# The opening of a two-layer backbone: chunk 0's copy, the low parts of the pooling weight, the residual's halves and the first gate weight in another order

## The chip, the core and the metric

The kernel runs on one core of a Trainium2 chip. The metric is the device time of one execution in microseconds (us). Three executions of the kernel before took 3039.23 to 3043.47 us, median 3042.01. One more was profiled.

## The reference, cut to what matters

Two layers over 256 latent tokens and 256 context tokens of 2048 channels, everything in float32. The opening of layer 0 is what the change touches:

```python
ml = (silu_c @ w_mod[i] + b_mod[i]).reshape(B, 6, 1, D)      # shift, scale, gate (mixer); shift, scale, gate (MLP)
a_lat = modulate(rms_norm(h, norm1_g[i]), ml[:, 0], ml[:, 1])
y_lat = pool_mix(a_lat, pool_w[j], pool_b[j], pool_scale[j]) # layer 0; layer 1 is neighbourhood attention
h = h + ml[:, 2] * y_lat
h = h + ml[:, 5] * conv_ffn(modulate(rms_norm(h, norm2_g[i]), ml[:, 3], ml[:, 4]), w_gate, w_up, conv_w, conv_b, w_down)
```

`pool_mix` takes, in each of four groups of 512 channels, the mean over a window of 2, 4, 8 or 16 tokens less the token itself, multiplies it with the group's 512x512 weight, and adds a bias. The context goes the same way with its own modulation.

## The kernel before, in words

**Layout.** Channels lie on the 128 partitions, so an activation is 16 tiles of 128 channels, each with 256 latent columns (`hl`, stream 0) and 256 context columns (`hc`, stream 1). Every float32 product is made of three: a weight is cast into a high part (`h` at the end of its name) on ScalarE (ACT) and a low part (`l`, the rest) on VectorE (DVE), activations likewise, and TensorE (PE) sums high x high, high x low and low x high into one PSUM bank. `load` (L132) brings 128x1024 tiles of 512 KB through SyncE's DMA queue; `split` (L148, L150) makes the two parts. A staged tile takes one of 15, later 14, rooms in rotation, so that a load waits until the tile that had its room has been used up.

**Modulation.** `w_mod` of layer 0 comes in chunks of 512 outputs: chunks 0 to 3 are the mixer's shift, 4 to 7 its scale, 8 to 11 its gate, 12 to 15 the MLP's shift, 16 to 19 its scale. A chunk has eight tiles (`wm_8_2_1024` is the second half of group 2 of chunk 8). `mod_pe` multiplies each tile on TensorE (L184, 32 columns at a time, four rows of the profile for one tile), copies the bank out on ACT (L191, `modev`), transposes it (L196, `modt`), and VectorE sums it (L199), adds the bias (L170) and, for scales, multiplies with the norm's gain (L172). The result is a column of numbers per chunk, `modT`.

**The first group's mixer.** `mixer(0)` makes the pooled rows `pf` of four tiles before the modulation is known (L567, L575, L576), casts the pooling weight (`parts = ld(wp[0], ...)`), multiplies the rows with chunk 4's scale on ACT (L625) and adds chunk 0's shift on VectorE (L626), and splits them (`ph`: L580 on ACT, L581 on VectorE). TensorE then makes 4 x 4 x 3 = 48 products of 512 columns (L588 to L590) into four banks, `pm_0` to `pm_3`. With chunk 8 known (`gsc`, `gbi`, L647 and L649), each bank is scaled (L663 on VectorE for the latent half, L666 on ACT for the context half) and added to the stream (L668, on VectorE or GpSimd). With chunk 16 known, the stream becomes the MLP's input `Ad` (L678 on ACT, L679 on VectorE).

**The gate and up products.** `partial(g, ...)` multiplies the four `Ad` tiles of group g with the first eight column tiles of the gate and up weights: `cg_0` to `cg_7`, `cu_0` to `cu_7` (L742 to L744), with small products for the shifts (`pw`, L698). The first gate weight `wcg_0` is loaded and split ahead, as `ahead`. Between the products, `between` calls `need`, which lets the loads and products of further chunks be recorded, and steps the mixer of the next group.

**What sets the order.** The program is recorded by generators that are stepped by hand (the loop over `(0, 8, 11, 13, 17, 17, 17)`: `need(n)` records the products of chunks up to a count of groups, `next(mix)` records the next piece of the mixer), and a scheduler then lays the instructions on each engine's queue by their priority and their own readiness in its model. Within an engine, and on SyncE's queue, instructions go in the order so fixed. `tc.issue_after(x)` keeps instructions behind x, `tc.high_priority()` moves them ahead.

## Time and profile before

| what | value |
|---|---|
| median of 3 runs | 3042.01 us |
| the profiled execution | 3042.44 us |
| its span, first to last instruction | 3040.7 us |
| TensorE busy | 2972.1 us, 98% |
| VectorE busy | 2054.5 us, 68% |
| ACT busy | 1347.4 us, 44% |
| HBM read | 563.32 MB, 189 GB/s over the span |

Rows of the timeline read: start, length, engine, line, operation, what is written and read, shape, how many, and in brackets how long the engine stood idle before and what released it. Rows of the chain of waits have start, length and name. A row of the waits gives the total, the number and the longest. A window's row gives the busy time of TensorE, its weight loads, VectorE, ACT and GpSimd, then the granted TensorE clock, the DMA share and GB/s. Times count from the first instruction.

### The profile page before, as it was taken

The page shows a single profiled execution, that of the slowest core. Times are in us where ns is not written, and L with a number is a line of the kernel's source. Part 1 is how long each engine was busy: PE and PEld are TensorE (multiplying, and loading weights), DVE is VectorE, ACT ScalarE, POOL GpSimd, SP SyncE. Part 2 cuts the span into 40 slices and gives each one's busy share as a digit, 9 for nine tenths or more (in the row PEclk, how much of TensorE's full clock was granted, in tenths as well). Part 3 has the DMA queues.
Part 4 walks back from the last instruction along what each step waited for, and adds up shares of the span by engine and source line. Part 5 has one row for each costly group of instructions (what it writes and reads, how often), then busy time and mean ns, then how long its engine had stood idle before and what let it go on. Part 6 is the DMA issues. An engine that isn't in the chain of part 4 may idle for free.

```text
span 3040.7 us, 40895 instructions
## 1 busy us (share of the span) xinstructions
PE 2972.1 (98%) x14846; PEld 2399.2 (79%) x14846; DVE 2054.5 (68%) x2894; ACT 1347.4 (44%) x2205; POOL 884.4 (29%) x868
## 2 busy tenths in 40 slices
PE   6999999999999999999999999999999999999998
PEld 2565678887888888888887888888888888888887
DVE  5445887576876867587686666474867666666666
ACT  3333473323334232333334444343546666566665
POOL 1111320303213030322413111010102566566665
PEclk9999999999999999999999999999999999999999
DMA  9878635454866857676783333333355555555563
GB/s 376 326 279 322 218 97 171 157 185 157 254 195 193 260 174 243 201 235 205 215 240 101 112 109 109 103 113 104 112 165 181 180 192 191 192 181 189 183 195 113
DMA packets 224778, 572.31 MB, mean 188 GB/s; under 512 B 55232, under 2 KB 68032, under 8 KB 224576
## 3 DMA queue, kind: packets, MB, share of 16 engines
q1 hardware_dynamic: 224576, 569.70, 58.0%
q8 instruction: 117, 1.92, 0.3%
q14 instruction: 85, 0.70, 0.1%
HBM read 563.32 MB, written 11.53 MB: 189 GB/s over the span
## 4 chain that ended last, share of the span: by engine, by line
PE 89%; issue 3%; DVE 3%; DMA 2%; ACT 1%; POOL 1%; SPq 0%; DVEq 0%; ACTq 0%; POOLq 0%
PE g L1018 5%; PE u L1018 5%; PE d L900 5%; PE d L902 5%; PE d L901 5%; PE d L1068 4%; PE u L865 4%; PE u L863 4%; PE u L864 4%; PE g L865 4%; PE g L864 4%; PE g L863 4%; PE u L1021 3%; PE g L1021 3%; PE d L1072 2%
## 5 line engine op out<-in xcount | busy, mean ns | idle before, releaser
L921 POOL TENSOR_TENSOR hl<-hl,dy 128x256 f32<-128x256 f32 x144 | 146.2, 1015 | 941.8 <-ACT dy L918 676.8
L1085 POOL TENSOR_TENSOR hl<-hl,dy 128x256 f32<-128x256 f32 x320 | 327.1, 1057 | 188.5 <-ACT dy L1083 186.2
L270 DVE SCALAR_TENSOR_TENSOR macc<-wm,sc,macc 128x512 f32<-128x512 f32 x360 | 262.3, 780 | 9.0 <-DMA wm<-wmod 8.9
L248 DVE SCALAR_TENSOR_TENSOR macc<-wm,sc,macc 128x1024 f32<-128x1024 f32 x120 | 160.4, 1336 | 87.3 <-DMA wm<-wmod 86.1
L918 ACT ACTIVATE dy<-d,modT 128x256 f32<-128x256 f32 x224 | 93.6, 471 | 138.6 <-PE d L902 134.7
L921 POOL TENSOR_TENSOR hc<-hc,dy 128x256 f32<-128x256 f32 x144 | 141.4, 982 | 0.0
L1261 POOL COPY bias<-rows 128x160 f32<-128x160 f32 x64 | 37.1, 579 | 306.2 <-issue 195.6
L1083 ACT ACTIVATE dy<-d,modT 128x512 f32<-128x512 f32 x160 | 104.5, 684 | 42.8 <-PE d L1072 41.3
L184 PE MATMUL mod<-wm,sc 128*32 128x512 f32 x640 | 101.6, 616 | 21.2 <-DVE n1q L353 18.9
L150 DVE TENSOR_TENSOR wd_2l<-wd,wd_2h 128x1024 fp32r<-128x1024 f32 (+1 forms) x44 | 58.6, 1343 | 60.5 <-ACT wd_2h L148 60.5
L488 ACT ACTIVATE sg<-g 128x512 f32<-128x512 f32 x43 | 27.3, 634 | 146.0 <-DVE g L485 145.9
L150 DVE TENSOR_TENSOR wd_3l<-wd,wd_3h 128x1024 fp32r<-128x1024 f32 (+1 forms) x44 | 54.5, 1262 | 52.7 <-ACT wd_3h L148 52.7
L575 POOL TENSOR_TENSOR pf<-ws,inv 128x256 f32<-128x256 f32 x32 | 27.9, 894 | 204.4 <-DVE ws L567 131.9
L148 ACT CAST wd_0h<-wd 128x1024 fp32r<-128x1024 f32 (+1 forms) x44 | 45.3, 1032 | 79.5 <-PE g L864 51.0
L150 DVE TENSOR_TENSOR wd_1l<-wd,wd_1h 128x1024 fp32r<-128x1024 f32 (+1 forms) x44 | 55.3, 1259 | 31.6 <-ACT wd_1h L148 31.6
L184 PEld LDWEIGHTS mod<-wm,sc 128*32 128x32 f32 x640 | 18.4, 109 | 65.1 <-issue 32.7
L1044 DVE TENSOR_TENSOR actb<-sgb,actb 128x256 fp32r<-128x256 f32 x43 | 52.9, 1229 | 23.7 <-ACT actb L1043 23.7
L900 PE MATMUL d<-act,wd_0h 128*128 128x512 f32 x172 | 67.4, 395 | 1.0 <-ACT dy L918 1.0
L900 PE MATMUL d<-act,wd_3h 128*128 128x512 f32 x172 | 68.2, 396 | 0.0
L901 PE MATMUL d<-act,wd_2h 128*128 128x512 f32 x172 | 68.1, 396 | 0.0
L150 DVE TENSOR_TENSOR wd_0l<-wd,wd_0h 128x1024 fp32r<-128x1024 f32 (+1 forms) x44 | 53.8, 1226 | 21.0 <-ACT wd_0h L148 21.0
L902 PE MATMUL d<-act,wd_0l 128*128 128x512 f32 x172 | 67.9, 395 | 0.0
(1708 smaller groups left out, 9381.7 us busy)
## 6 DMA issues: line engine op xcount, KB each, us to landing
wm<-wmod SPq DMA_DIRECT2D x384, 512.0 KB, 6.2
wd<-wd SPq DMA_DIRECT2D x168, 512.0 KB, 4.5
wg<-wg SPq DMA_DIRECT2D x156, 512.0 KB, 4.6
wu<-wu SPq DMA_DIRECT2D x156, 512.0 KB, 4.5
wv<-wv SPq DMA_DIRECT2D x32, 512.0 KB, 3.7
wk<-wq SPq DMA_DIRECT2D x32, 512.0 KB, 3.7
wq<-wq SPq DMA_DIRECT2D x32, 512.0 KB, 3.7
wo<-wo SPq DMA_DIRECT2D x32, 512.0 KB, 4.4
```

The lines of the kernel that those rows point to most:

```text
L150: eng.tensor_tensor(lo[:, :n], t[:, :n], hi[:, :n].bitcast(F32), op=ALU.subtract)
L270: nc.vector.scalar_tensor_tensor(acc[:, s], w, sc2[:, k, s : s + 1], acc[:, s], op0=ALU.mult, op1=ALU.add)
L863: nc.tensor.matmul(ps, hi[:, c : c + P], xh, start=(k == 0), stop=False)
L864: nc.tensor.matmul(ps, hi[:, c : c + P], xl, start=False, stop=False)
L865: nc.tensor.matmul(ps, lo[:, c : c + P], xh, start=False, stop=(k == KT - 1))
L900: nc.tensor.matmul(ps, hi[:, o : o + P], xh, start=(i == 0), stop=False)
L901: nc.tensor.matmul(ps, hi[:, o : o + P], xl, start=False, stop=False)
L902: nc.tensor.matmul(ps, lo[:, o : o + P], xh, start=False, stop=(i == n - 1))
L921: nc.gpsimd.tensor_tensor(h_of(s)[:, k, :], h_of(s)[:, k, :], y[:, s], op=ALU.add)
L1018: nc.tensor.matmul(ps, hi[:, c : c + P], flat(B[k]), start=(k == 0), stop=False)
L1021: nc.tensor.matmul(ps[:, T:], lo[:, c : c + P], B[k][:, 0], start=False, stop=(k == KT - 1))
L1085: nc.gpsimd.tensor_tensor(hl[:, k, :], hl[:, k, :], y[:, q], op=ALU.add)
```

## The change

It does five things, all in the opening of layer 0:

1. The late pooled rows (tiles 2 and 3, L625) are issued on ACT only after the copy of chunk 0.
2. The low parts of the first pooling weight are made on VectorE after the last low part of the pooled rows, and TensorE's 48 products come as 32 with the weight's high part, then 16 with its low part.
3. The residual's second half (`pm_2`, `pm_3`) is recorded directly after the first (the fifth step asks for 13 groups, not 17).
4. The first gate weight is loaded as two tiles of 512 KB at two places. Its first part is split before chunk 16's copy and sum, which are kept behind it (the copy behind the cast on ACT, the sum behind the low part on VectorE); its second part is split behind chunk 16's copy and the last low part of `Ad`.
5. Nothing else is edited, but the scheduler lays out what follows anew, as far as group 2.

```diff
-    def split(ts, name, share=0):
+    def split(ts, name, share=0, lows=None):
...
-                nc.scalar.copy(hi[:, :n], t[:, :n])
+                cast = nc.scalar.copy(hi[:, :n], t[:, :n])
...
+                if lows is None:
+                    low = eng.tensor_tensor(lo[:, :n], t[:, :n], hi[:, :n].bitcast(F32), op=ALU.subtract)
+                    made[:] = [cast.ins, low.ins]
+                else:
+                    lows.append((lo, t, hi))
...
+    def behind(ch, j):
+        return tc.issue_after(first_split[j]) if ch == 16 else ExitStack()
...
-                    with tc.high_priority() if ch in (0, 4, 8, 16) else ExitStack():
-                        nc.scalar.copy(ev, ps)
+                    with tc.high_priority() if ch in (0, 4, 8, 16) else ExitStack(), behind(ch, 0):
+                        copied[ch] = nc.scalar.copy(ev, ps).ins
...
+                with behind(ch, 1):
+                    nc.vector.tensor_reduce(out=r, in_=by_row(p2, 2 * c), axis=AX.X, op=ALU.add)
...
-                    parts = ld(wp[0], "wp0")
+                    lows = []
+                    parts = split(load(lambda a, b: wp[0][:, a:b], 2048, "wp0"), "wp0", lows=lows)
...
-                            nc.scalar.activation(v, v, AF.Copy, scale=M(0, 1, k, s))
+                            with tc.issue_after(copied[0]) if k > 1 else ExitStack():
+                                nc.scalar.activation(v, v, AF.Copy, scale=M(0, 1, k, s))
...
+                    with tc.issue_after(low_done[-1]):
+                        for lo, t, hi in lows:
+                            nc.vector.tensor_tensor(lo, t, hi.bitcast(F32), op=ALU.subtract)
...
-                            pool_mm(banks[m], parts, pa, i, m)
+                            pool_mm(banks[m], parts, pa, i, m, (True, False))
+                    for i in range(4):
+                        for m in range(4):
+                            pool_mm(banks[m], parts, pa, i, m, (False, True))
...
-            for n in (0, 8, 11, 13, 17, 17, 17):
+            for n in (0, 8, 11, 13, 13, 17, 17):
...
-                    ahead.append(load(lambda a, b: wg[0, a // 512 : b // 512, :, 0:512].rearrange("f p c -> p f c"), 2048,
-                                      "wcg0_0"))
+                    ahead.append(load(lambda a, b: wg[0, 0:2, :, 0:512].rearrange("f p c -> p f c"), 1024, "wcg0_0"))
                     ahead.append(split(ahead[0], "wcg0_0"))
+                    first_split[:] = made
                 need(n)
+                if n == 17 and len(ahead[0]) == 1:
+                    ahead[0] += load(lambda a, b: wg[0, 2:4, :, 0:512].rearrange("f p c -> p f c"), 1024, "wcg0_1")
                 next(mix)
+            hold[:] = [copied[16], low_done[-1]]
+            ahead[1] += split(ahead[0][1:], "wcg0_1")
+            hold.clear()
```

What this moves shows in the order of each engine's instructions (line, operation, what is written and read; the change shifts line numbers, so L625 becomes L643, L626 L644, L581 L595, L150 L153 or L648). First VectorE between the last pooled row and TensorE's first pooling products, before:

```order
L576 TENSOR_TENSOR pf_252<-pf_252,pad_221 128x512
L150 TENSOR_TENSOR wp0l_351<-wp_0_346,wp0h_350 128x1024
L199 TENSOR_REDUCE modT_0_363<-modt_358 128x8
L170 TENSOR_TENSOR modT_0_363<-modT_0_363,vt 128x8
L150 TENSOR_TENSOR wp0l_355<-wp_1024_348,wp0h_354 128x1024
L626 SCALAR_TENSOR_TENSOR pf_237<-z,modT_0_363,pf_237 128x256 x4
L626 SCALAR_TENSOR_TENSOR pf_252<-z,modT_0_363,pf_252 128x256 x4
L581 TENSOR_TENSOR ph_395<-pf_237,ph_395 128x512
```

And after:

```order
L588 TENSOR_TENSOR pf_252<-pf_252,pad_221 128x512
L211 TENSOR_REDUCE modT_0_361<-modt_356 128x8
L176 TENSOR_TENSOR modT_0_361<-modT_0_361,vt 128x8
L644 SCALAR_TENSOR_TENSOR pf_237<-z,modT_0_361,pf_237 128x256 x4
L644 SCALAR_TENSOR_TENSOR pf_252<-z,modT_0_361,pf_252 128x256 x4
L595 TENSOR_TENSOR ph_393<-pf_237,ph_393 128x512
L595 TENSOR_TENSOR ph_400<-pf_237,ph_400 128x512
L595 TENSOR_TENSOR ph_407<-pf_252,ph_407 128x512
L595 TENSOR_TENSOR ph_414<-pf_252,ph_414 128x512
L648 TENSOR_TENSOR wp0l_351<-wp_0_346,wp0h_350 128x1024
L648 TENSOR_TENSOR wp0l_354<-wp_1024_348,wp0h_353 128x1024
```

Both low parts went from ahead of the shift (`modT_0`) to behind the split rows. Then ACT around the residual, before:

```order
L191 COPY modev_427<-mod_366 128x512
L666 ACTIVATE pz_500<-pm_0_446,gbi_230,gsc_229 128x256
L666 ACTIVATE pz_505<-pm_1_447,gbi_230,gsc_229 128x256
L148 CAST wcg_0h_530<-wcg_0_0_526 128x1024
L148 CAST wcg_0h_534<-wcg_0_1024_528 128x1024
L191 COPY modev_546<-mod_437 128x512
L666 ACTIVATE pz_566<-pm_2_448,gbi_230,gsc_229 128x256
L666 ACTIVATE pz_571<-pm_3_449,gbi_230,gsc_229 128x256
L678 ACTIVATE Ad_576<-hl,modT_16_553 128x256
```

And after:

```order
L202 COPY modev_427<-mod_364 128x512
L690 ACTIVATE pz_500<-pm_0_446,gbi_230,gsc_229 128x256
L690 ACTIVATE pz_505<-pm_1_447,gbi_230,gsc_229 128x256
L690 ACTIVATE pz_510<-pm_2_448,gbi_230,gsc_229 128x256
L690 ACTIVATE pz_515<-pm_3_449,gbi_230,gsc_229 128x256
L150 CAST wcg_0h_538<-wcg_0_0_536 128x1024
L202 COPY modev_550<-mod_437 128x512
L702 ACTIVATE Ad_572<-hl,modT_16_557 128x256
```

The four steps of the residual stand together, one cast is left ahead of chunk 16's copy (`modev_550`), and the other has gone behind the `Ad` steps. Last TensorE some 80 products later, where the gate products of group 0 meet chunk 9 (`mod_904`), before:

```order
L184 MATMUL mod_904<-wm_9_1_0_928,sc 32x512 x2
L742 MATMUL cg_5_921<-Ad_586,wcg_4h_867 128x512
L743 MATMUL cg_5_921<-Ad_586,wcg_4h_867 128x512
L744 MATMUL cg_5_921<-Ad_586,wcg_4l_868 128x512
L184 MATMUL mod_904<-wm_9_1_1024_930,sc 32x512 x2
L742 MATMUL cg_5_921<-Ad_591,wcg_4h_867 128x512
L743 MATMUL cg_5_921<-Ad_591,wcg_4h_867 128x512
L744 MATMUL cg_5_921<-Ad_591,wcg_4l_868 128x512
L744 MATMUL cg_971<-Ad_576,wcg_4l_872 128x512
L742 MATMUL cg_971<-Ad_581,wcg_4h_871 128x512
L184 MATMUL mod_904<-wm_9_2_0_963,sc 32x512 x2
```

And after:

```order
L769 MATMUL cg_1009<-Ad_587,wcg_4l_872 128x512
L195 MATMUL mod_904<-wm_9_0_0_905,sc 32x512 x2
L195 MATMUL mod_904<-wm_9_0_1024_907,sc 32x512 x2
L195 MATMUL mod_904<-wm_9_1_0_928,sc 32x512 x2
L195 MATMUL mod_904<-wm_9_1_1024_930,sc 32x512 x2
L195 MATMUL mod_904<-wm_9_2_0_963,sc 32x512 x2
L195 MATMUL mod_904<-wm_9_2_1024_965,sc 32x512 x2
L195 MATMUL mod_904<-wm_9_3_0_999,sc 32x512 x2
L195 MATMUL mod_904<-wm_9_3_1024_1001,sc 32x512 x2
L767 MATMUL cu_1203<-Ad_572,wcu_4h_1062 128x512
```

Chunk 9's tiles, single ones between gate products before, are one run of eight behind all gate products of group 0. Counted in the same way over the whole order from the first gate product to chunk 14, chunks' products stand in 33 runs before and in 28 after. In the pooling itself it is the other way round: chunk 8's eight tiles stand there as one pair and four single tiles before (the first pair ahead of it), as seven single tiles after (one ahead of it). On SyncE's queue the second part of the first up weight (`wcu_0_1024`) moved ten places back, behind most of chunk 5, and chunk 9's first two tiles moved behind chunk 17's first two.

More of the change, by code (lines that the diff above doesn't have):

```diff
@@ L107 @@
     hold = []
+    made = []
+    first_split = []
     RING = {"wst": 3, "wm": 2, "wa": 1}
@@ L174, in finish_mod @@
         modT[l, ch] = mt
+    copied = {}
+    def behind(ch, j):
+        return tc.issue_after(first_split[j]) if ch == 16 else ExitStack()
     def mod_pe(chs, sc, pool):
@@ L576, in pooled @@
                 nc.vector.tensor_tensor(pf, pf, pad[:, :, PAD : PAD + T], op=ALU.subtract)
+            low_done = []
             def parts_of(pf, k):
@@ L580, in parts_of, with pool_mm @@
                 nc.scalar.copy(ph[:, 0], pf)
-                nc.vector.tensor_tensor(ph[:, 1], pf, ph[:, 0].bitcast(F32), op=ALU.subtract)
+                low_done.append(nc.vector.tensor_tensor(ph[:, 1], pf, ph[:, 0].bitcast(F32), op=ALU.subtract).ins)
                 return ph
-            def pool_mm(ps, parts, pa, i, m):
+            def pool_mm(ps, parts, pa, i, m, which=(True, True)):
                 hi, lo = parts[i // 2]
@@ L587, in pool_mm @@
                 rh, rl = flat(pa[i][:, 0]), flat(pa[i][:, 1])
-                nc.tensor.matmul(ps, hi[:, c : c + P], rh, start=(i == 0), stop=False)
-                nc.tensor.matmul(ps, hi[:, c : c + P], rl, start=False, stop=False)
-                nc.tensor.matmul(ps, lo[:, c : c + P], rh, start=False, stop=(i == 3))
+                if which[0]:
+                    nc.tensor.matmul(ps, hi[:, c : c + P], rh, start=(i == 0), stop=False)
+                    nc.tensor.matmul(ps, hi[:, c : c + P], rl, start=False, stop=False)
+                if which[1]:
+                    nc.tensor.matmul(ps, lo[:, c : c + P], rh, start=False, stop=(i == 3))
             def mixer(g):
```

7 lines of the change are left out of this document (3 added, 4 removed).

## The prediction

> **What bounds the kernel now.** I read the page first, then the waits of TensorE, then the opening in order of time. The page:
>
> ```profile
> span 3040.7 us, 40895 instructions
> PE 2972.1 (98%) x14846; PEld 2399.2 (79%) x14846; DVE 2054.5 (68%) x2894; ACT 1347.4 (44%) x2205; POOL 884.4 (29%) x868
> ```
>
> TensorE is busy for 98% of the span. Anything that shortens the end must either take idle time of TensorE away or make its own stream shorter. The profiled execution took 3042.44 us with a span of 3040.7 us; its time is 0.4 us above the median of the three runs, 3042.01 us, so a sum against it serves for both. Where TensorE stands still between 39 and 90 us, its waits say:
>
> ```profile
> PE modt L196 <- ACT modev L191: 4.8, 3, 2.6
> PE cg L742 <- ACT Ad L678: 3.3, 1, 3.3
> PE pm L588 <- ACT ph L580: 1.7, 1, 1.7
> ```
>
> So 9.8 us of idle time lie in the stretch that the change rewrites. The same stretch by windows (busy time, granted clock, DMA share, GB/s at the end of a row):
>
> ```profile
> 42.80:46.80 4.00, 2.29 (x8) 0.19 (x4) 3.96 (x8) 1.38 (x2) 0.00 (x0) 0.50 1.02 404
> 46.80:53.10 6.30, 6.29 (x18) 3.31 (x19) 4.08 (x9) 1.85 (x3) 0.00 (x0) 0.50 1.02 406
> 53.10:67.00 13.90, 13.90 (x59) 7.72 (x58) 0.00 (x0) 0.59 (x1) 0.00 (x0) 1.00 1.03 405
> 77.00:80.40 3.40, 3.09 (x7) 2.49 (x8) 3.16 (x8) 2.65 (x7) 0.00 (x0) 0.50 1.01 397
> ```
>
> Two things are to be seen: after each long stop TensorE runs some microseconds at half clock, and the transfers are saturated there, 512 KB in about 1.3 us (524,288 bytes at 404 to 406 GB/s).
>
> **Part 1, chunk 0's copy and the pooling weight's low parts.** The opening in order of time (start, length):
>
> ```profile
> 38.04 1.05 PE L184 MATMUL mod<-wm,sc 128*32 128x512 f32 x4 [0.23 <-DMA wm<-wmod]
> 40.29 0.91 ACT L625 ACTIVATE pf<-pf,modT 128x256 f32<-128x256 f32 x2 [0.91 <-DVE pf L576]
> 41.10 0.56 ACT L191 COPY modev<-mod 128x512 f32<-128x512 f32 x1
> 41.57 1.99 ACT L148 CAST wp0h<-wp 128x1024 fp32r<-128x1024 f32 x2
> 41.72 0.66 PE L196 MATMUL modt<-ident,modev 128*128 128x128 f32 x4 [2.63 <-ACT modev L191]
> 42.64 1.23 DVE L150 TENSOR_TENSOR wp0l<-wp,wp0h 128x1024 fp32r<-128x1024 f32 x1 [2.39 <-ACT wp0h L148]
> 44.09 1.22 DVE L150 TENSOR_TENSOR wp0l<-wp,wp0h 128x1024 fp32r<-128x1024 f32 x1
> 45.23 3.25 DVE L626 SCALAR_TENSOR_TENSOR pf<-z,modT,pf 128x256 f32<-128x256 f32 x8
> 46.14 0.62 ACT L580 CAST ph<-pf 128x512 fp32r<-128x512 f32 x1 [2.58 <-DVE pf L626]
> 46.81 2.08 PE L588 MATMUL pm<-ph,wp0h 128*128 128x512 f32 x4 [1.72 <-ACT ph L580]
> 48.40 2.49 DVE L581 TENSOR_TENSOR ph<-pf,ph 128x512 fp32r<-128x512 f32 x4
> ```
>
> Chunk 0's products end at 38.04 + 1.05 = 39.09 us, its copy starts at 41.10. Put ahead of the late rows it runs 39.1 to 39.7, and the transposes end at 40.4. The rows held back (four steps, two groups of 0.91) then take ACT to 41.5, and the two casts, 1.99, to 43.5: as before, so the wait that the change adds costs nothing there. VectorE no longer has 2.5 us of low parts ahead of L626: the sum and bias take 0.4 us, L626 runs from 40.9 to 44.2. ACT is what is late next: the first ph cast ends at 43.5 + 0.6, and TensorE starts pooling at 44.2 instead of 46.81, **2.6 us earlier**. L581 then ends at 46.7 and the low parts at 49.2; TensorE asks for them only after 32 of its 48 products, so they are covered by 9 us and more of products. Were that cover gone, the price would be at most their 2.5 us.
>
> Not all of this survives, since the order of TensorE now has seven lone tiles of chunk 8 between the pooling products, against one pair and four lone ones before. A lone tile's price stands in the chain:
>
> ```profile
> 125.57 0.98 PE mod L184 x4
> 126.55 0.43 PE cg L742
> 126.98 0.23 PE cg L743
> ```
>
> It is 0.98 and a first product that takes 0.43 instead of 0.23: 1.18 us. From 44.2 I let the clock be half for 5.5 us (bounds from the windows: 3.4 as at 77 us, 6.3 as at 46.8). In them go four products (2.08), a tile (1.3, my estimate) and five products at 0.43 (a product at half clock: 3.09 / 7 in the last window above is 0.44). Left are 39 products at 0.23 and six tiles at 1.18, 16.1 us: the end is at 65.8 against 66.75, **0.95 us earlier**. With the clock's bounds it is 0.5 to 2.0.
>
> [...]
>
> **Part 2, the residual's halves together and the gate weight in two places.**
>
> ```profile
> 66.75 0.60 PE L196 MATMUL modt<-ident,modev 128*128 128x128 f32 x4
> 67.28 3.64 PE L184 MATMUL mod<-wm,sc 128*32 128x512 f32 x32
> 67.38 0.19 DVE L199 TENSOR_REDUCE modT<-modt 128x8 f32<-128x32 f32 x1 [16.50 <-PE modt L196]
> 68.22 0.99 DVE L663 TENSOR_SCALAR pz<-pm,gsc,gbi 128x256 f32<-128x256 f32 x2
> 68.86 1.04 ACT L666 ACTIVATE pz<-pm,gbi,gsc 128x256 f32<-128x256 f32 x2 [5.32 <-DVE pz L663]
> 69.13 0.75 DVE L668 TENSOR_TENSOR hl<-hl,pz 128x256 f32<-128x256 f32 x2
> 69.50 1.67 POOL L668 TENSOR_TENSOR hc<-hc,pz 128x256 f32<-128x256 f32 x2 [29.97 <-ACT pz L666]
> 69.80 1.98 ACT L148 CAST wcg_0h<-wcg 128x1024 fp32r<-128x1024 f32 x2
> 71.68 0.58 ACT L191 COPY modev<-mod 128x512 f32<-128x512 f32 x1
> 75.61 0.65 DVE L172 SCALAR_TENSOR_TENSOR modT<-modT,vt 128x8 f32<-128x8 f32 x1
> 76.35 0.51 ACT L678 ACTIVATE Ad<-hl,modT 128x256 fp32r<-128x256 f32 x1 [1.45 <-DVE modT L172]
> 77.31 1.22 PE L742 MATMUL cg<-Ad,wcg_0h 128*128 128x512 f32 x2 [3.34 <-ACT Ad L678]
> ```
>
> With pooling's end 0.95 us earlier, the transposes start at 65.8, chunk 16's products run 66.3 to 70.0 and VectorE's sum of chunk 8 starts at 66.4. Four L663 at 0.49 then run from 67.3 to 69.2 and four ACT steps at 0.51 from 67.9 to 70.0; before, the second two of each came 5 us later, behind the two gate casts and their low parts. One cast, 1.0, ends at 71.0, and the copy of chunk 16, which now waits for it, runs to 71.6: TensorE's products were done at 70.0, so this added wait costs 1.0 us. Queued behind it on ACT are only the Ad steps, which need its result. VectorE has four additions at 0.37 and one low part (1.2) until 72.3, just when the transposes (0.66) end, so the sum's wait behind the low part costs nothing. Then come sum, bias and gain. They take 0.6 us at the durations that chunk 8's steps had (0.2 each), or 1.5 as at 74.9 to 76.35, where L172 took 0.65 beside GpSimd's additions. GpSimd's four additions, 0.84 each from 68.5, are over at 71.9, so I take 0.6: first Ad at 72.9, first gate product 0.96 later as before (76.35 to 77.31), at 73.9. That is **3.4 us earlier** than 77.31, part 1 included; 2.5 to 4.5 with the bounds.
>
> The second part's cast and low part stand behind the eight Ad steps (0.4 apart), so they end near 78.5. TensorE wants them after 24 gate products and chunk 12's tiles, past 84: hidden, with 5 us of cover.
>
> The longest stop of TensorE falls from 3.34 us to about 1.5, so I expect the spell at half clock at 77.0 to 80.4 to go. Seven products there took 0.43 instead of 0.23: **1.4 us** (bound 0, if the spell stays).
>
> **Part 3, TensorE's order behind it.** The rest is TensorE without a gap, and its length depends on how often products of chunks interrupt gate products. A pair of tiles in a run costs as follows, with the later stops that matter and a window of the stretch:
>
> ```profile
> 83.96 1.06 PE L184 MATMUL mod<-wm,sc 128*32 128x512 f32 x8
> PE mod L184 <- ACT modev L191: 0.7, 1, 0.7
> 258.98 0.73 PE L742 MATMUL cg<-Ad,wcg_0h 128*128 128x512 f32 x2 [0.28 <-ACT Ad L678]
> 260.57 0.50 PE L743 MATMUL cg<-Ad,wcg_0h 128*128 128x512 f32 x1 [0.86 <-DVE Ad L679]
> 130.00:330.00 200.00, 198.87 (x1090) 119.00 (x1087) 116.62 (x188) 65.81 (x114) 31.42 (x36) 1.00 0.84 309
> ```
>
> Eight rows (a pair) take 1.06 us, as long as the 1.05 of a lone tile above, and 32 rows (four pairs) 3.64: a further pair is (3.64 - 1.06) / 3 = 0.86, and each run costs 0.98 + 0.20 - 0.86 = 0.32 beside its pairs. From the first gate product to chunk 14 the order of before has 33 runs with 52 pairs (a lone tile counts as one), that of after 28 runs with 48. The gain is 4 x 0.86 + 5 x 0.32 = **5.0 us**, if the tiles have landed where they now stand together; if TensorE waits for them instead, 0. I take 5.0, since the transfers are busy for 0.84 there and TensorE is hardly ever waiting (198.87 of 200 us).
>
> Small terms: the stop of 0.7 us behind chunk 5's copy goes, for chunk 9 no longer follows it directly. Group 1 now has the order that group 2 had (transposes, all of chunk 13, gate products), where TensorE stood 0.28 + 0.86 = 1.1 us: lost. The first up shift is cut in two: one more restart, 0.3 with its 0.2 from the chain rows (my estimate). The reordered rows near 1669 and 2302 us issue the same instructions; I put them at 0, within 1 us either way.
>
> The sum: -3.4 - 1.4 - 5.0 - 0.7 + 1.1 + 0.3 = -9.1 us, 3042.4 - 9.1 = **3033.3 us**.
>
> **Rivals.** (1) *The merged runs wait for their tiles.* Chunk 9's eight tiles are now used at one place, and two of them are issued after chunk 17's first. For it: transfers were saturated up to 67 us; against it: 0.84 later. The 5.0 fall away: 3038.4.
>
> [...]
>
> (3) *Slower: SyncE's queue stops at a room.* SyncE issues in order; the second up part and chunk 9's first tiles need rooms that become free only when TensorE has passed the gate and up shifts, and every load behind them waits too. TensorE then stands before chunk 9's run. It decides from 9.1 us of lateness, seven transfers at 1.3. At ten transfers, 13 us, plus 1.4 for a new spell at half clock, it gives 3033.3 + 14.4 = 3047.7. Against it: TensorE has some 70 products of its own between the release and the use.
>
> **How the numbers follow.** Forecast 0.62, rival 1 0.20, rival 2 0.12, rival 3 0.06. A measurement of this kernel can tell about 0.2%, 6.1 us, from no change: faster means under 3035.9. Rival 2 and nine tenths of the forecast's cases lie there, 0.68; rival 1 and the rest are 0.26; rival 3 is 0.06. The range goes from the forecast with pooling, clock and the small terms at their good ends, or rival 2 with 2 us of spread, 3029, to rival 1 with the spell of 1.4 kept, 3040.
>
> **What would show it.** In the profile after, right if: pooling's first product is at 44 to 45 us and starts 2 to 3 us earlier; pooling ends at 64 to 66.5; the first gate product is at 73 to 75 with no row of clock 0.50 behind it; chunk 9's tiles are one run of about 3.6 us with no wait for a transfer; and TensorE's idle time behind 130 us grows by about 1 us. Wrong if TensorE waits for wm tiles by more than 3 us anywhere, if the chunk 16 copy starts after 73, or if the gain of the opening is there at 90 us and gone at 400.

## The result, and the profile after

The kernel after took 3036.89 us (median of 15 executions, 3031.15 to 3038.76), the kernel before 3043.24 in the same rounds (15 executions, 3038.22 to 3045.18). The ratio is 0.9978, 95% interval 0.9972 to 0.9985: 6.7 us less, with 4.6 to 8.5 by the interval. The forecast was 3033.3. The profiled execution took 3036.41 us with a span of 3034.6, against 3042.44 and 3040.7 before. The page:

```profile
span 3034.6 us, 40899 instructions
PE 2968.7 (98%) x14846; PEld 2399.5 (79%) x14846; DVE 2048.7 (68%) x2894; ACT 1346.7 (44%) x2205; POOL 880.8 (29%) x868
```

The same waits of TensorE as before (total, number, longest):

```profile
PE modt L207 <- ACT modev L202: 4.7, 6, 1.4
PE pm L603 <- ACT ph L594: 3.4, 1, 3.4
PE cg L767 <- ACT Ad L702: 2.9, 2, 1.9
```

The wait before the gate products is shorter, but the one before the pooling has doubled, where the prediction wanted it gone. Three of the windows that were shown of before (the last three numbers of a row are granted clock, DMA share and GB/s):

```profile
42.80:46.80 4.00, 0.57 (x3) 0.45 (x2) 3.43 (x11) 3.81 (x7) 0.00 (x0) 0.57 1.02 406
46.80:53.10 6.30, 6.30 (x21) 3.28 (x21) 4.93 (x7) 1.06 (x3) 0.00 (x0) 0.73 1.03 406
...
77.00:80.40 3.40, 3.40 (x10) 2.59 (x9) 2.95 (x8) 2.92 (x6) 0.00 (x0) 0.57 1.02 410
```

Both stretches at half clock are still there, the first one shorter. The opening in order of time:

```profile
30.45 0.58 ACT L529 COPY rs<-n1b 128x512 f32<-128x512 f32 x1 [11.40 <-PE n1b L394]
...
39.08 0.59 ACT L202 COPY modev<-mod 128x512 f32<-128x512 f32 x1 [0.43 <-PE mod L195]
...
42.99 0.91 ACT L643 ACTIVATE pf<-pf,modT 128x256 f32<-128x256 f32 x2 [0.91 <-DVE pf L588]
...
46.35 2.07 PE L603 MATMUL pm<-ph,wp0h 128*128 128x512 f32 x4 [3.43 <-ACT ph L594]
...
76.64 0.73 PE L767 MATMUL cg<-Ad,wcg_0h 128*128 128x512 f32 x2 [1.88 <-ACT Ad L702]
...
250.22 3.64 PE L195 MATMUL mod<-wm,sc 128*32 128x512 f32 x32
```

In the profile before, the first and the last of these stand so:

```profile
27.74 0.59 ACT L517 COPY rs<-n1b 128x512 f32<-128x512 f32 x1 [8.45 <-PE n1b L382]
...
255.06 3.64 PE L184 MATMUL mod<-wm,sc 128*32 128x512 f32 x32
```

Chunk 0's copy runs at 39.08, as forecast. But the norm's result (`rs`), from which the pooled rows are made, was copied 2.71 us later in this execution, ahead of everything that the change touches, and the late pooled rows hold ACT until 43.9. So the pooling starts at 46.35 instead of 46.81, and the first gate product comes at 76.64 instead of 77.31: 0.67 us. Behind it the gain grows: chunk 14's run (32 rows) begins at 250.22 instead of 255.06, 4.84 earlier, and the span is 6.1 shorter.

Two questions follow: does the gain come from TensorE's order behind the opening, or from the opening itself; and was the late norm the change's doing?

### The profile page after: what moved, and what is told of

Same layout as the page of the kernel before. It is cut to its first block, busy times and chain, and to the rows that moved or that the text cites. A ratio compares the mean times of both kernels' runs of the same rounds, so it can differ in the third digit from the quotient of the medians.

```text
span 3034.6 us, 40899 instructions
## 1 busy us (share of the span) xinstructions
PE 2968.7 (98%) x14846; PEld 2399.5 (79%) x14846; DVE 2048.7 (68%) x2894; ACT 1346.7 (44%) x2205; POOL 880.8 (29%) x868
## 4 chain that ended last, share of the span: by engine, by line
PE 90%; issue 4%; DVE 3%; ACT 1%; POOL 1%; DMA 1%; SPq 0%; DVEq 0%; ACTq 0%; POOLq 0%
PE g L1048 5%; PE u L1048 5%; PE d L930 5%; PE d L932 5%; PE d L931 5%; PE d L1098 4%; PE u L895 4%; PE u L893 4%; PE u L894 4%; PE g L895 4%; PE g L894 4%; PE g L893 4%; PE g L1051 3%; PE u L1051 3%; PE d L1102 2%
## 5 line engine op out<-in xcount | busy, mean ns | idle before, releaser
L1113 ACT ACTIVATE dy<-d,modT 128x512 f32<-128x512 f32 x160 | 104.4, 683 | 43.1 <-PE d L1102 41.5
L153 DVE TENSOR_TENSOR wd_2l<-wd,wd_2h 128x1024 fp32r<-128x1024 f32 (+1 forms) x44 | 58.6, 1343 | 61.0 <-ACT wd_2h L150 61.0
L153 DVE TENSOR_TENSOR wd_3l<-wd,wd_3h 128x1024 fp32r<-128x1024 f32 (+1 forms) x44 | 54.8, 1269 | 52.3 <-ACT wd_3h L150 52.3
L150 ACT CAST wd_0h<-wd 128x1024 fp32r<-128x1024 f32 (+1 forms) x44 | 45.3, 1032 | 79.1 <-PE g L894 49.3
L153 DVE TENSOR_TENSOR wd_1l<-wd,wd_1h 128x1024 fp32r<-128x1024 f32 (+1 forms) x44 | 55.2, 1258 | 31.1 <-ACT wd_1h L150 31.1
L153 DVE TENSOR_TENSOR wd_0l<-wd,wd_0h 128x1024 fp32r<-128x1024 f32 (+1 forms) x44 | 55.0, 1252 | 20.7 <-ACT wd_0h L150 20.7
L932 PE MATMUL d<-act,wd_2l 128*128 128x512 f32 x172 | 67.9, 395 | 0.0
```

Of the source, the lines that this page charges most:

```text
L153: low = eng.tensor_tensor(lo[:, :n], t[:, :n], hi[:, :n].bitcast(F32), op=ALU.subtract)
L932: nc.tensor.matmul(ps, lo[:, o : o + P], xh, start=False, stop=(i == n - 1))
```

## The experiments

All ratios are to the kernel before, executed on the same chip beside the kernel named. A spell is a stretch in which TensorE's granted clock is 0.50. "The split" is the gate weight's split in two places.

**The split alone, and all but the split.** The first keeps only this of the change (line numbers aside), and with it that chunk 16's copy and sum stay behind the first part's cast and low part:

```diff
-ahead.append(load(lambda a, b: wg[0, a // 512 : b // 512, :, 0:512].rearrange("f p c -> p f c"), 2048, "wcg0_0"))
+ahead.append(load(lambda a, b: wg[0, 0:2, :, 0:512].rearrange("f p c -> p f c"), 1024, "wcg0_0"))
...
+ahead[0] += load(lambda a, b: wg[0, 2:4, :, 0:512].rearrange("f p c -> p f c"), 1024, "wcg0_1")
...
+hold[:] = [copied[16], low_done[-1]]
+ahead[1] += split(ahead[0][1:], "wcg0_1")
```

Expected: 

> Of the change, only the first gate weight in two tiles at two places is kept; copy, low parts and residual stand as before. TensorE's order behind chunk 8 is then that of the kernel after, five runs and four pairs of tiles fewer than before, while the pooling stands as before. Theory A (the gain is TensorE's shorter order behind the opening): first gate product within 1.5 us of before's 77.3, then 4 to 5 us gained between 89 and 250 us; time 3038 to 3040, ratio to before 0.9983 to 0.9990. Theory B (the gain is the waits of the opening, the later order is incidental): at most 1 us gained, 3042 or more, ratio 0.9996 or more. Theory C (the differences are where the half-clock spells fall): no checkpoint moves by over 1 us in this run except where a spell moves, ratio within 0.001 of 1.

Measured: 3035.74 us (median of 11), ratio 0.9979 (0.9970 to 0.9988). The whole gain is there: theory A, with a time below its 3038 to 3040. Its opening is even later than before's:

```profile
31.35 0.59 ACT L529 COPY rs<-n1b 128x512 f32<-128x512 f32 x1 [11.49 <-PE n1b L394]
50.42 2.07 PE L603 MATMUL pm<-ph,wp0h 128*128 128x512 f32 x4 [2.11 <-ACT ph L594]
78.76 1.22 PE L759 MATMUL cg<-Ad,wcg_0h 128*128 128x512 f32 x2 [2.86 <-ACT Ad L694]
```

The first gate product is 1.45 us behind before's, and chunk 14's run (252.10) 2.96 ahead of it: 4.4 us were gained between the two. The second undoes just the split, and with it the place of chunk 16's copy and sum:

```diff
-ahead.append(load(lambda a, b: wg[0, 0:2, :, 0:512].rearrange("f p c -> p f c"), 1024, "wcg0_0"))
+ahead.append(load(lambda a, b: wg[0, a // 512 : b // 512, :, 0:512].rearrange("f p c -> p f c"), 2048, "wcg0_0"))
...
-hold[:] = [copied[16], low_done[-1]]
-ahead[1] += split(ahead[0][1:], "wcg0_1")
...
-        return tc.issue_after(first_split[j]) if ch == 16 else ExitStack()
+        return ExitStack()
```

Expected: 

> The change without the gate weight's split: copy ahead, low parts last, residual halves together; one gate weight tile pair, loaded and split as before. TensorE's later order is that of before (same runs and pairs). Theory A: the opening gives at most 1 us by 90 us and nothing behind it; 3041.5 to 3043.5, ratio 0.9994 to 1.0001. Theory B: first gate product 2 to 3.5 us earlier than 77.3 and the lead is kept to the end: 3038 to 3040.5, ratio 0.9984 to 0.9991.

Measured: 3040.59 us (median of 11), ratio 1.0000 (0.9991 to 1.0009): theory A. Yet its profile has an opening that is 2.3 us earlier than before's, and chunk 14's run at 251.45, 3.6 earlier:

```profile
28.16 0.59 ACT L529 COPY rs<-n1b 128x512 f32<-128x512 f32 x1 [8.38 <-PE n1b L394]
44.48 2.04 PE L603 MATMUL pm<-ph,wp0h 128*128 128x512 f32 x4 [0.23 <-ACT ph L594]
74.99 0.74 PE L767 MATMUL cg<-Ad,wcg_0h 128*128 128x512 f32 x2 [2.08 <-ACT Ad L702]
```

**Is the late norm of the execution or of the change?** The kernel before and the kernel after, unchanged, were profiled once more.

Expected of the kernel before: 

> The kernel before, profiled once more. Theory F (the norm's copy at 27.74 in before's profile against 30.45 in after's is a matter of the execution, not of the change): the norm's copy comes anywhere from 27.7 to 31.4, and the pooling starts 19.1 us behind it within 0.3, the first gate product 47.3 to 49.7 behind it by the spells. Rival (the change itself makes the norm late): 27.5 to 28.2 again. Time as before, ratio 0.9990 to 1.0010.

Expected of the kernel after: 

> The kernel after, once more, in the same company as the next three. Theory A2 (the split of the gate weight brings the gain through TensorE's later order; the opening's gain of the copy is eaten by lone tiles in the pooling and by where the half-clock spells fall): ratio to before 0.9972 to 0.9985 again; counted from the copy of the norm's result the pooling starts 15.9 us later within 0.3, whatever the norm's own start does, and the first gate product 44.5 to 47 us later, by the spells that happen to fall there. Theory C (every checkpoint moves freely from execution to execution): these two distances move by over 1 us beside the spells.

Measured: before again 3041.95 us, ratio 1.0001 (0.9992 to 1.0010); after again 3036.26, ratio 0.9972 (0.9960 to 0.9983). Before, once more:

```profile
22.28 3.58 PE L366 MATMUL n1s<-ones,n1q 128*128 128x1 f32 x16
30.12 0.59 ACT L517 COPY rs<-n1b 128x512 f32<-128x512 f32 x1 [10.61 <-PE n1b L382]
49.19 2.07 PE L588 MATMUL pm<-ph,wp0h 128*128 128x512 f32 x4 [2.11 <-ACT ph L580]
78.25 0.73 PE L742 MATMUL cg<-Ad,wcg_0h 128*128 128x512 f32 x2 [3.34 <-ACT Ad L678]
```

The same kernel has its norm at 27.74 in one execution and at 30.12 in another, so the late norm is a matter of the execution (theory F), and the pooling follows 19.07 us behind it both times. After again had the norm at 30.30 and the pooling 15.91 behind (15.90 the first time), as theory A2 has it. The opening must therefore be counted from the norm's copy. What differs in the executions is seen in the norm's sums, `n1s`, which are issued just ahead: 3.58 us here and in the profile after, against

```profile
21.98 2.11 PE L366 MATMUL n1s<-ones,n1q 128*128 128x1 f32 x16
```

in the first profile of before. The clock column reads 1.00 in both, but it has no row of another value yet; in the combined kernel below it reads 0.54 and 0.50 there, and the sums take 3.58. The trace's first record of the clock, at 1.00, stands at 22.36 us in the first profile of before, early in the sums, and at 28.50 (before again) and 29.67 (after) behind them. So I take the late norm for one at half clock.

**How long the spells at half clock are** is the other thing that differs. Windows cut at their edges, of the first profile of before, of the profile after, and of the kernel without the split:

```profile
42.80:53.00 10.20, 8.48 (x26) 3.40 (x23) 8.05 (x16) 3.23 (x5) 0.00 (x0) 0.50 1.02 406
53.10:56.00 2.90, 2.90 (x15) 1.76 (x13) 0.00 (x0) 0.00 (x0) 0.00 (x0) 1.00 1.04 406
```

```profile
43.40:50.10 6.70, 3.75 (x8) 1.35 (x8) 6.31 (x13) 4.46 (x8) 0.00 (x0) 0.50 1.03 408
50.20:56.00 5.80, 5.80 (x26) 3.21 (x24) 1.53 (x2) 0.00 (x0) 0.00 (x0) 1.00 1.03 406
```

```profile
42.90:46.30 3.40, 3.17 (x8) 1.16 (x4) 3.40 (x9) 3.13 (x6) 0.00 (x0) 0.51 1.05 411
46.40:53.00 6.60, 6.60 (x29) 3.36 (x28) 3.66 (x5) 0.00 (x0) 0.00 (x0) 1.00 1.02 406
```

They last about 3.4, 6.8 or 10.2 us, one, two or three times the same length: 10.2, 6.7 and 3.4 here, and 3.4 or 10.2 for the later ones in the clock's records of the first profile of before and of the profile after, but for one at the end of each span. The same kernel has them differently from execution to execution: over the pooling the granted clock of before was 0.84 the first time and 0.91 the second. In two of these three profiles the fall had no long stop ahead of it: in the profile after, the clock had fallen by 43.4, half a microsecond into the stop of 3.43 us and with none above 1.5 between the norm's copy and it, and in the kernel without the split it fell by 42.9 with stops of 1.5 us at most. What sets the length and the place of a spell no run shows.

**The accounts of all kernels.** From here each profile is counted from its norm's copy, with the loss at half clock taken off: (1 - granted clock) x length, from a window over the pooling (first to last product's start) and one over the first 14 us of gate products. For the kernels before, after and without the split these windows are:

```profile
46.81:66.52 19.71, 19.71 (x72) 10.63 (x72) 4.08 (x9) 2.44 (x4) 0.00 (x0) 0.84 1.03 405
77.31:91.31 14.00, 13.21 (x62) 7.74 (x63) 5.19 (x14) 6.56 (x17) 0.00 (x0) 0.89 0.73 259
```

```profile
46.35:67.34 20.99, 20.99 (x75) 10.00 (x76) 5.38 (x8) 2.09 (x4) 0.00 (x0) 0.91 1.03 405
76.64:90.64 14.00, 13.26 (x59) 7.89 (x60) 5.42 (x12) 7.03 (x17) 0.00 (x0) 0.88 0.76 267
```

```profile
44.48:64.55 20.07, 20.07 (x76) 9.96 (x77) 5.58 (x9) 2.14 (x4) 0.00 (x0) 0.95 1.03 404
74.99:88.99 14.00, 13.21 (x68) 7.58 (x68) 5.91 (x15) 6.58 (x17) 0.00 (x0) 1.00 0.89 329
```

For before: pooling 19.71 - 0.16 x 19.71 = 16.6; norm to first gate product 49.57 - 3.15 = 46.4; from there to chunk 14's run 177.75 - 0.11 x 14 = 176.2. All kernels so (us; the last two columns compare the account with the time):

| kernel | norm's copy | to pooling | pooling | its last to first gate product | norm to gate product | gate product to chunk 14 | account against before | measured ratio (interval) |
|---|---|---|---|---|---|---|---|---|
| before | 27.74 | 19.07 | 16.6 | 10.8 | 46.4 | 176.2 | | |
| before again | 30.12 | 19.07 | 16.6 | 10.8 | 46.5 | 176.3 | +0.2 | 1.0001 (0.9992-1.0010) |
| after | 30.45 | 15.90 | 19.1 | 9.3 | 44.3 | 171.9 | -6.4 | 0.9978 (0.9972-0.9985) |
| after again | 30.30 | 15.91 | 19.1 | 9.3 | 44.3 | 171.9 | -6.4 | 0.9972 (0.9960-0.9983) |
| split alone | 31.35 | 19.07 | 16.6 | 9.6 | 45.4 | 171.8 | -5.5 | 0.9979 (0.9970-0.9988) |
| all but the split | 28.16 | 16.32 | 19.1 | 10.4 | 45.8 | 176.5 | -0.3 | 1.0000 (0.9991-1.0009) |
| copy alone | 27.80 | 16.38 | 17.6 | 10.8 | 44.7 | 175.9 | -2.0 | 0.9998 (0.9989-1.0007) |
| all but the low parts | 31.32 | 15.90 | 17.6 | 9.3 | 42.8 | 169.6 | -10.3 | 0.9969 (0.9958-0.9981) |
| additions on VectorE | 30.75 | 15.91 | 19.1 | 9.0 | 44.0 | 172.0 | -6.7 | 0.9965 (0.9953-0.9978) |
| fillers | 31.11 | 15.91 | 19.1 | 9.6 | 44.6 | 169.8 | -8.3 | 0.9961 (0.9949-0.9974) |
| fillers, low parts as before | 30.75 | 15.91 | 17.6 | 9.6 | 43.1 | 171.9 | -7.7 | 0.9965 (0.9951-0.9978) |
| products ahead of the norm | 29.32 | 16.20 | 19.1 | 9.3 | 44.6 | 172.0 | -6.1 | 0.9972 (0.9962-0.9983) |
| combined | 30.15 | 15.91 | 17.5 | 9.9 | 43.3 | 169.9 | -9.5 | 0.9967 (0.9954-0.9979) |

In every row the account lies inside the interval or at its edge (0.1% is 3.0 us). It also shows why the kernel without the split led by 3.6 us in its profile and had no gain in its times: 3.15 - 1.0 us of the lead are the shorter spell in the pooling, and 1.5 the missing spell behind the gate product. These are the execution's, not the kernel's; 0.3 is left, less 0.4 by which its norm was later.

The account ends at chunk 14's run. From there to the end of the span the two profiles of before took 2785.6 and 2783.4 us and the two of after 2784.4 and 2784.0, so behind it no gain or loss of the change can be seen; the lead of 4.84 us that became 6.1 in the first pair lies within that spread.

**The copy alone, and all but the low parts.** The copy ahead (`issue_after(copied[0])` on L642) is kept and the rest undone; in the second kernel only the low parts' move is undone:

```diff
-parts = split(load(lambda a, b: wp[0][:, a:b], 2048, "wp0"), "wp0", lows=lows)
+parts = ld(wp[0], "wp0")
...
-                    with tc.issue_after(low_done[-1]):
-                        for lo, t, hi in lows:
-                            nc.vector.tensor_tensor(lo, t, hi.bitcast(F32), op=ALU.subtract)
```

with the 48 products as before. Expected of the copy alone: 

> Of the change only the copy of chunk 0 ahead of the late pooled rows; low parts, residual and gate weight as before, and TensorE's later order as before. Theory G (the copy alone brings the earlier pooling, the explicit move of the low parts adds only lone tiles): pooling's start 15.9 us behind the norm's copy within 0.3 (19.1 before), pooling 17.5 us long at full clock, the first gate product 2 to 3 us earlier behind the norm's copy than in the kernel before with the same spells; ratio 0.9988 to 0.9997. Rival 1 (the low parts ahead are the cause, as the prediction's part 1 put it): start 17.5 to 18.5 behind the norm's copy, ratio 0.9995 to 1.0003. Rival 2 (nothing of the opening reaches the end): start as in theory G and yet ratio 0.9998 or more, as in the run without the split.

Expected of all but the low parts: 

> The change without the low parts' move: the pooling weight's low parts are made with its casts, the 48 products stand as before. The later order is a little shorter than that of the kernel after (one run and one pair fewer, 1.2 us at 0.86 and 0.32), and the pooling holds a run of three tiles and four lone ones, 1.5 us shorter than seven lone tiles at 1.18. Theory A: the later order keeps its gain and adds 1.2; the pooling starts up to 2.5 us later and is 1.5 shorter: 3035 to 3037.5, ratio 0.9974 to 0.9982, no worse than the kernel after. Theory B: the low parts ahead give back 2 to 2.5 us: 3039 to 3040, ratio 0.9986 to 0.9990.

Measured: copy alone 3039.82 us, ratio 0.9998 (0.9989 to 1.0007); all but the low parts 3033.03, ratio 0.9969 (0.9958 to 0.9981), better than its theory A's 0.9974 to 0.9982. In the profile of the copy alone:

```profile
27.80 0.59 ACT L529 COPY rs<-n1b 128x512 f32<-128x512 f32 x1 [8.31 <-PE n1b L394]
39.54 0.59 ACT L202 COPY modev<-mod 128x512 f32<-128x512 f32 x1 [3.54 <-PE mod L195]
40.03 1.70 ACT L642 ACTIVATE pf<-pf,modT 128x256 f32<-128x256 f32 x4
41.82 3.26 DVE L643 SCALAR_TENSOR_TENSOR pf<-z,modT,pf 128x256 f32<-128x256 f32 x8 [0.55 <-ACT pf L642]
44.18 1.98 PE L603 MATMUL pm<-ph,wp0h 128*128 128x512 f32 x4
44.99 2.35 DVE L153 TENSOR_TENSOR wp0l<-wp,wp0h 128x1024 fp32r<-128x1024 f32 x2
```

With the norm at 27.80 the pooling starts at 44.18, and the low parts (L153) fall behind the shift (L643) by themselves, with no edit that puts them there. So no run has the copy ahead and the low parts still in front of the shift, and rival 1 of its expectation, which counted on that, is not tested. The distance of 16.38, where theory G had 15.9 within 0.3, goes with an early norm: the late rows (L642) stand directly behind the copy here, where in the profile after they came later and waited for VectorE (42.99, `DVE pf`). In the three kernels with the copy ahead whose norm came before 30 us it is 16.2 to 16.4, in the others 15.9. The move of the low parts adds nothing to the start (15.90 with and without it) and costs 1.5 us in the pooling, 19.1 against 17.6: seven lone tiles against a run of three and four lone ones. The ratio of the copy alone, 0.9998, is the one that rival 2 of its expectation gave, and above theory G's 0.9988 to 0.9997; yet it cannot tell the account (-2.0) from rival 2, for the interval, -3.3 to +2.1 us, holds both.

Without the low parts' move the later order is shorter as well, by 2.3. One run and one pair fewer make 0.32 + 0.86 = 1.2; 1.0 more are two stops of the kernel after which that order does not have:

```profile
162.34 0.66 PE L207 MATMUL modt<-ident,modev 128*128 128x128 f32 x4 [0.39 <-ACT modev L202]
167.85 0.50 PE L768 MATMUL cg<-Ad,wcg_0h 128*128 128x512 f32 x1 [0.59 <-DVE Ad L703]
```

**VectorE's additions.** In the profile after, four additions of the residual took 3.09 us on VectorE, where the prediction had 4 x 0.37:

```profile
70.32 3.35 POOL L692 TENSOR_TENSOR hc<-hc,pz 128x256 f32<-128x256 f32 x4 [28.09 <-ACT pz L690]
70.86 3.09 DVE L692 TENSOR_TENSOR hl<-hl,pz 128x256 f32<-128x256 f32 x4
73.10 0.65 PE L207 MATMUL modt<-ident,modev 128*128 128x128 f32 x4 [1.36 <-ACT modev L202]
73.87 1.21 DVE L153 TENSOR_TENSOR wcg_0l<-wcg,wcg_0h 128x1024 fp32r<-128x1024 f32 x1
75.01 0.18 DVE L211 TENSOR_REDUCE modT<-modt 128x8 f32<-128x32 f32 x1
```

The sum of chunk 16 waits for its transposes until 73.75 and then for the low part until 75.01: 1.3 us. The experiment puts the context half on VectorE too:

```diff
-eng = nc.vector if g == 0 and s == 0 else nc.gpsimd
+eng = nc.vector if g == 0 else nc.gpsimd
```

Expected: 

> The kernel after with the context half of the residual's additions on VectorE too, so that GpSimd adds nothing beside it: eight additions on VectorE instead of four. Theory E (VectorE's four additions take 0.77 us each beside GpSimd's four of 0.84, and 0.37 alone): eight additions at 0.37 to 0.41 each, 3.0 to 3.3 us, so that the low part and the first gate product come when they came: 46 to 46.5 us behind the norm's copy, ratio as after, 0.9972 to 0.9985. Rival (they are slow by themselves there, by their operands or by waits for ACT): 0.77 each, 6.2 us, first gate product 3 us later, ratio 0.9982 to 0.9995.

Measured: 3032.48 us (median of 5), ratio 0.9965 (0.9953 to 0.9978). The first and the last of its additions, and the low part behind them:

```profile
71.15 0.75 DVE L692 TENSOR_TENSOR hl<-hl,pz 128x256 f32<-128x256 f32 x2
73.16 0.75 DVE L692 TENSOR_TENSOR hc<-hc,pz 128x256 f32<-128x256 f32 x2
73.83 1.22 DVE L153 TENSOR_TENSOR wcg_0l<-wcg,wcg_0h 128x1024 fp32r<-128x1024 f32 x1
```

Eight additions run from 71.15 to 73.91, 0.35 each, in less time (2.76 us) than four beside GpSimd (3.09). Theory E holds for the additions: the four are slow because GpSimd adds beside them. The first gate product comes only 0.3 us sooner by the account (44.0 against 44.3), since the low part now stands behind eight additions. One after the other the eight of the profile after, four on each engine, would take 4 x 0.74 + 4 x 0.35 = 4.4 us (an estimate; 0.74 is the median of GpSimd's additions in the profile after, 0.35 is from this run). That trace has both done 3.6 us after the first start (70.32 to 73.95), so by it they ran side by side for a part of the time; GpSimd's spans are rough. How GpSimd slows VectorE there no run shows.

**Fillers in TensorE's stops.** Products whose results nobody uses (ones and the identity) behind chunk 0's and chunk 16's transposes, 12 and 10:

```diff
+    def fillers(ins, n):
+        fb = bank("d", "fill")
+        with tc.issue_after(ins):
+            for _ in range(n):
+                nc.tensor.matmul(fb[:, 0:128], ones, ident, start=True, stop=True)
```

Expected: 

> The kernel after with extra products on TensorE (ones and the identity, 128x128, results unused): 12 behind chunk 0's transposes and 10 behind chunk 16's, about 2.0 and 1.7 us at 0.165 each, in stops of 3.4 and 1.9 us. The later order has one pair of tiles fewer (0.9 us). Theory D (the stops before the pooling and before the gate products are what sends the clock to half there, 1.9 us and 1.4 us in the profile after): no row of clock 0.50 between 42 and 82 us, 2 to 4 us under the kernel after: ratio 0.9964 to 0.9972. [...] Rival (the fillers delay chunk 8's first tile and the pooling): pooling's start over 16.5 us behind the norm's copy, ratio 0.9978 to 0.9985.

Expected with the low parts as before: 

> As e6_fill, but without the low parts' move: the 48 pooling products stand as before, with a run of three tiles and four lone ones between them instead of seven lone ones. Theory A2: the pooling is 1.5 us shorter than in e6_fill and the later order 0.9 longer: 0.5 to 1 us under e6_fill, within what the rounds can tell; against the kernel after 3 to 4 us less if the fillers hold the clock (ratio 0.9962 to 0.9970), 0.5 to 1 us less if they don't (0.9972 to 0.9978). Theory B' (low parts behind the split rows help the start): pooling's start 1 us or more later behind the norm's copy than in e6_fill.

Measured: 3033.85 us, ratio 0.9961 (0.9949 to 0.9974), and 3034.22, ratio 0.9965 (0.9951 to 0.9978). The windows of the first:

```profile
47.02:67.74 20.72, 20.72 (x76) 9.79 (x76) 5.39 (x8) 2.10 (x4) 0.00 (x0) 0.92 1.03 404
77.32:91.32 14.00, 13.26 (x68) 6.95 (x64) 6.45 (x15) 7.24 (x18) 0.00 (x0) 1.00 1.00 344
```

Theory D falls for the pooling: 0.92, as in after again. Behind the gate product no spell came in any of the three kernels with fillers, but none came either in two kernels that have the split and no filler there (all but the low parts, additions on VectorE), so that this stays open. Over all 13 profiles such a spell came in four of four with a stop of 2.9 or 3.3 us ahead of the first gate product, in three of six with a stop of 1.6 to 2.1, and in none of the three with fillers. The medians are 2.4 and 2.0 us below after again, and the account gives other reasons for it: in the first the scheduler laid out the later order without the stops at 162 and 168 us, as without the low parts' move (169.8), and in the second the pooling is 1.5 us shorter.

**Products ahead of the norm, and the combination.** 60 such products ahead of the norm, in the kernel after; then 44 of them with 8 and 10 fillers, the additions on VectorE and the low parts as before.

Expected of the 60: 

> The kernel after, with 60 extra products of ones and the identity (128x128, results unused) recorded ahead of the norm, so that TensorE works from about 3.5 us on until the first tile lands at 18.8. Theory A: the part of the opening's gain that is missing was lost because TensorE ran at half clock until 29.7 us in the profiled run (22.4 in before's); at full clock the norm's sums (n1s) take 2.1 us instead of 3.58, its result is copied at 27.7 instead of 30.45, the late pooled rows come 2.7 us earlier and the pooling starts at 43.5 to 44.5 instead of 46.35; time 2 to 3 us under the kernel after, 3034 to 3035, ratio to before 0.9969 to 0.9974, and the times spread less. Rival: the pooling's start is bound elsewhere (transfers, VectorE's rows), it stays at 45.5 to 46.5, time as after, 0.9975 to 0.9981. Rival C: if the clock is not raised by such products, n1s stays at 3.6 and the products only delay chunk 4 by up to 2 us: ratio 0.9978 to 0.9985.

Expected of the combination: 

> The kernel after without the low parts' move, with all eight of the residual's additions on VectorE, and with extra products on TensorE (results unused): 44 ahead of the norm, 8 behind chunk 0's transposes, 10 behind chunk 16's. Later order: as many runs as after, one pair fewer. If the single gains add: pooling 1.5 shorter, later order 0.9, no spell at half clock between 40 and 82 us (2 to 3 against a mean of after), 1 to 2 from the norm: 5 to 7 us under the kernel after, ratio to before 0.9950 to 0.9962. Rival (the spells only move, and what is gained in one place is lost in another): 2 to 4 us under it, 0.9962 to 0.9972.

Measured: 3033.51 us, ratio 0.9972 (0.9962 to 0.9983), and 3031.67, ratio 0.9967 (0.9954 to 0.9979). With 60 the norm's sums take 1.95 us, but a spell comes right behind them (granted clock 0.87 and 0.70 in the windows 22 to 26 and 26 to 30 us), and the pooling starts at 45.52, neither the 43.5 to 44.5 expected nor the rival's. In the combination the 44 did not help:

```profile
18.00:22.00 4.00, 2.74 (x8) 0.41 (x8) 3.55 (x7) 1.61 (x6) 0.00 (x0) 0.54 1.03 410
22.00:26.00 4.00, 4.00 (x22) 3.68 (x24) 0.08 (x1) 0.00 (x0) 0.00 (x0) 0.50 1.02 405
```

Its ratio lies in its rival's range (0.9962 to 0.9972): in the times the single gains don't add up. Both it and the change without the low parts' move, which needs no extra product, are faster than the kernel before. That they are faster than the kernel after is not shown by the times, whose intervals overlap with 0.9972 to 0.9985; only the accounts say so (-9.5 and -10.3 against -6.4). The two cannot be told apart.

## Why the prediction was right or wrong

- **The size.** The sum was -9.1 us; the account of the kernel after has -6.4, the measurement -6.7. The measured time lies inside the range, 3.6 us above the forecast, and the forecast's gain lies outside the interval of 4.6 to 8.5. The measured time is 1 us above the 3035.9 that the working set for faster, which went by three executions of before; against the 3043.24 measured beside it, it is faster by a little over 0.2%.
- **Part 1, the start, was right, but the move of the low parts was not needed for it.** The forecast was the pooling at 44.2; with a norm at 27.80 and the copy ahead it starts at 44.18, by the steps of the working (late rows until 41.7, forecast 41.5). The working gave VectorE's low parts as what stood in the way, and in the profile before they did. They are out of the way as soon as the copy is ahead, and the explicit move of them gave nothing. How much of the 3.2 us is the copy's and how much the low parts' was not separated.
- **Part 1, the pooling's length, was right too.** Lone tiles were priced as a loss, and they are: 16.6 us to 19.1 at full clock. Start and length leave 3.2 - 2.5 = 0.7 us. The forecast was 0.95, but 0.4 of it was a spell taken at 5.5 us instead of 6.3.
- **Part 2 failed in the step "VectorE has four additions at 0.37 and one low part (1.2) until 72.3, just when the transposes (0.66) end, so the sum's wait behind the low part costs nothing".** Beside GpSimd the four take 3.09; the price of 0.37 came from additions that had begun ahead of GpSimd's (69.13 against 69.50). The low part ends at 75.08, and the sum waits 1.26 us for it. From the pooling's last product to the first gate product 1.5 us were gained; the working had 2.45.
- **The term of 1.4 us for the spell at 77 us failed.** A stop of 1.9 instead of 3.3 was to end the spell. It came in both profiles of after and with the 60 products, and was missing in three other kernels with stops of 1.6 to 2.1. With such stops it came in three profiles of six, so that its staying in the profile after is chance, as its going would have been. The spells change from execution to execution (a granted clock of 0.84 and of 0.91 over the pooling of the kernel before), so they should have been a spread on both sides, not a term.
- **Part 3 was right, and carries most of the gain.** Runs and pairs at 0.32 and 0.86, with the small terms, made 5.0 + 0.7 - 1.1 - 0.3 = 4.3 us; measured from the first gate product to chunk 14's run, 176.2 - 171.9 = 4.3. The stop of group 1 is 0.39 + 0.59 = 1.0, forecast 1.1. Behind chunk 14's run the two stops of 0.28 and 0.86 became one of 1.06, which changes next to nothing. That sum and measurement agree to 0.1 us is luck; that the split alone has 176.2 - 171.8 = 4.4 as well, with the same order, is not.
- **What the working did not say** is which edit makes part 3. It is the split, and it alone carries nearly the whole change (0.9979); the copy, the residual's halves and the low parts together come to nothing that can be measured without it (1.0000). Why the scheduler then lays out the later order so, and whether the two places or the place of chunk 16's copy and sum do it, no run separates.
- The terms close: -9.1 + 1.4 (spell) + 0.95 (part 2) + 0.3 (part 1) = -6.45.
- **The signs.** The merged run came, with no wait for a transfer, and the stops behind 130 us grew by 0.39 + 0.59 + 1.06 - 0.28 - 0.86 = 0.9 us, as said. The signs in absolute time did not come in the profile after: the pooling starts at 46.35 and ends past 67.3, the first gate product is at 76.64, and a spell goes with it. The norm of this execution was 2.71 us late, and the working counted from the first instruction.

Rival 1 fell: chunk 9's run stands in one piece and waits for no tile.

```profile
130.04 3.64 PE L195 MATMUL mod<-wm,sc 128*32 128x512 f32 x32
```

The 0.12 of rival 2, and what the range's 3029 takes from it, stand for a pooling at full clock, which no run shows: over the pooling the granted clock was 0.84 to 0.95 in all 13 profiles. Rival 3 fell with rival 1.

## What to carry to other kernels

Count an opening from the last thing that the change does not touch, here the norm's copy, and take the loss at half clock off before two profiles are compared: two profiles of the kernel before differed by 2.4 us in the first and, over the pooling, by 1.5 in the second. An edit that lets the scheduler lay out TensorE anew is priced by counting its interruptions, over the whole stretch that moves; here that was worth more than every wait that the edits were about. A move that lets other work break up a dense run of products (the low parts last, seven lone tiles) can cost more than the wait it removes.

## What the runs showed of the hardware

- Spells at half clock lasted about 3.4, 6.8 or 10.2 us, and the same kernel had a granted clock of 0.84 over its pooling in one execution and of 0.91 in another. A stop of 1.9 us before the gate products was followed by one in three profiles (granted clock 0.88 over the first 14 us of gate products) and in another by none (1.00).
- The norm's sixteen sums of one column take 1.95 to 2.11 us or 3.58, and with them the norm's copy comes at 27.7 to 28.2 us or at 30.1 to 31.4, in kernels with the same order up to there; only with 60 products ahead was it 29.32.
- Four additions of 128x256 on VectorE took 3.09 us beside four on GpSimd, and eight alone 2.76.
